# Delta recurrence: applying the inverse to (r - Kg S) in each step instead of forming the product of Kg and the inverse

## The chip, the cores and the metric

The kernel runs on one core of a Trainium2 chip, as one program. The metric is the device time of one execution in microseconds, taken as the median over several runs. A core has a matrix engine (TensorE, "PE" in the profile, whose weight loads are listed apart as "PEld"), a vector engine (VectorE, "DVE"), a scalar engine (ScalarE, "ACT"), GpSimd ("POOL") and SyncE ("SP"), which here only starts DMA transfers. In this kernel every engine works through its own instructions in the order in which the program wrote them, and the engines wait for each other through semaphores. The products stand in PSUM until VectorE or ScalarE takes them away.

## The reference

One decoder layer with three gated branches is computed for a prompt of 1024 tokens and for 8 decode tokens. From h = RMSNorm(x) one wide projection (1024 to 7688 columns) feeds a gated delta-rule branch, a spatial-gating branch and a cross-attention branch; each is projected back, gated and merged, and an output projection, a residual and a norm follow. The change is in the delta-rule branch. Its chunked form, cut to what matters here:

```python
L = where(strict, einsum('id,jd->ij', k_beta, k) * decay, 0.0)
Tinv = triangular_solve(eye + L, eye)           # the inverse
u = Tinv @ (v * beta)
w = Tinv @ (k_beta * exp(gc))
attn = where(causal, q @ k.T * decay, 0.0)
def step(S, xs):                                # over the chunks, S is the state
    v_new = u_i - w_i @ S
    o = qd_i @ S + attn_i @ v_new
    S = S * gl_i + kd_i.T @ v_new
    return S, o
```

There are 4 heads with keys and values of 128 columns. Since u - w S = Tinv (v beta - (k beta exp(gc)) S), the inverse may be applied before or after the difference is formed.

## The kernel before

All activations are kept transposed: features on partitions, tokens along the free dimension. The projections are products of 128x128 weight blocks with 344 tokens, done three times (high x high, high x low, low x high part) for accuracy. A *job* is one block of 128 output features: `w_next` takes its split weights and starts the load of the block three jobs ahead, then three groups follow (`h_group`, `mm3`, L272 to L282), each of 24 matmuls into one of two PSUM banks ("pj"), and each group's result is taken away, mostly by ScalarE (L957).

The order of the work is written by hand. The class `Streams` holds side streams, which are Python generators. `mm3` calls `tick` after every sixth matmul, and a tick advances each side stream to its next `yield`; `yield n` lets n more ticks pass first. So the instructions of side streams come to stand between the matmuls of the projections, in the order of the ticks. `plan_a` (L205 to L210) lists the jobs of the first stage: k, v and q of head 0, then more of branch A and B and some gates, up to the last gate of head 3's row. The recurrence is the side stream `delta_all` (L949): `gates_gen`, then `delta_gen(h)` for the heads 0 to 3, one after the other. After the last job of `plan_a` stands `run.until(lambda: ("delta", 3) in done)` (L994), which ticks on without any matmuls until head 3 has ended. Only then the next stage is written: loads of the memory input and of small tables on SP's queue (L1010 to L1026), `mem_norm` (L291), and the jobs of `plan_c`, which begins with two gates, a gate and the first w_mem_kv block.

`delta_gen(h)` works in 8 chunks of 128 tokens. It transposes k by chunks (L756 to L766) and, out of the same PSUM tiles, forms Kg = k exp(gc) with tokens on partitions; it forms the decayed products LA (L780), the right-hand side r from v (L810), and the transposes of q for its norm (L817); `gcb` holds exp(gc) over tokens along the free dimension, and L827 turns it into q exp(gc). GpSimd inverts the small diagonal blocks (L835), and TensorE with VectorE builds the whole inverse U from them (L854 to L888). Then come the product of Kg and U (L890 to L896) and the recurrence over chunks (L900 to L922): y, the new state Sn, and the output. After the chunks the output is normed (L924 to L931), transposed back (L935), gated, and stored to `ya_d` (L946).

The scaling of beta and of the norms is folded into other factors: r, kd and LA carry them.

Of the kernel before, what the change touches and what calls it, by code (L numbers as in the profile page):

```python
# [12 lines left out]
F32 = mybir.dt.float32  # L13
F32R = mybir.dt.float32r
I32 = mybir.dt.int32
AF = mybir.ActivationFunctionType
ALU = mybir.AluOpType
AX = mybir.AxisListType
PSUM = bass.MemoryType.PSUM
DRAM = bass.MemoryType.DRAM  # L20

P = 128
D = 1024
T = 1024
# [5 lines left out]
H = 4  # L30
CC = 8
# [59 lines left out]


class Streams:
    """Interleaves the emission of side streams (generators) with the main stream of matrix products."""

    def __init__(self):
        self.items = []
# [21 lines left out]
def tile_mixer_step(ctx: ExitStack, tc: tile.TileContext, a):  # L119
    nc = tc.nc  # L120
    V, S, G, PE, SP = nc.vector, nc.scalar, nc.gpsimd, nc.tensor, nc.sync
# [25 lines left out]
    def dl():  # L147
        return ps.tile([P, 512], F32, tag="dl", name="dl", bufs=4)
# [41 lines left out]
        p = in_.shape[0]  # L190
        PE.transpose(out, in_, ident[:p, :p])  # L191

    # ---- weights: loaded three jobs ahead, split one job ahead
    w_in_v = a["w_in"].rearrange("(k p) n -> p k n", p=P)
    w_kv_v = a["w_mem_kv"].rearrange("(k p) n -> p k n", p=P)
    w_br_v = [a[n].rearrange("(k p) n -> p k n", p=P) for n in ("w_br_a", "w_br_b", "w_br_c")]
# [90 lines left out]
        for n in range(NS):  # L287
            evac(n, *h_group(w, n))

    # ---- RMSNorm of the inputs, transposed and split  # L290
    def mem_norm(np_, srcs, g_bc, dst_h, dst_l):  # L291
        ss = np_.tile([P, 2], F32, tag="nss", name="mss")
        r = np_.tile([P, 2], F32, tag="nrs", name="mrs")
# [168 lines left out]

    run.add(norm_gen())

    # ---- scratch in DRAM for branch parts that wait for their turn
    ya_d, bv_d, ug_d, yc_d, yb_d = (
        [dr.tile([P, NT], F32, name=f"{n}{h}") for h in range(H)] for n in ("ya", "bv", "ug", "yc", "yb")
    )
# [5 lines left out]
    def bc4(x):  # L474
        return x.unsqueeze(2).to_broadcast([P, x.shape[1], P])

    # ---- branch A
    dst = ExitStack()
    kq_t, v_t, kq_s = {}, {}, {}
    xraw = {}  # L480
# [59 lines left out]
    for n in range(4):  # L540
# [10 lines left out]
    dp = scoped(dst, "dp")  # L551
# [3 lines left out]
        out=mask, in_=mask, pattern=[[1, P]], compare_op=ALU.is_ge, fill=NEG, base=0, channel_multiplier=-1  # L555
# [3 lines left out]
        out=ut, in_=ones, pattern=[[1, P]], compare_op=ALU.is_ge, fill=0.0, base=0, channel_multiplier=-1  # L559
# [4 lines left out]
    U = dp.tile([P, CC, P], F32, name="U")  # L564
# [5 lines left out]
    beta = dp.tile([P, H, 9], F32, name="beta")  # L570
    g = dp.tile([P, H, 9], F32, name="g")
    gc = dp.tile([P, H, CC], F32, name="gc")
    eg = dp.tile([P, H, CC], F32, name="eg")
    egl = dp.tile([P, H, CC], F32, name="egl")
    ekd = dp.tile([P, H, CC], F32, name="ekd")
    gcd = dr.tile([32, P], F32, name="gcd")
# [12 lines left out]
    def gates_gen():  # L589
        sel = dp.tile([16, 8], F32, name="sel")  # L590
        V.tensor_tensor(out=sel, in0=ident[:16, 0:8], in1=ident[:16, 8:16], op=ALU.add)
        yield
        t = tp()
        for i in range(9):
            PE.matmul(t[:, i * 8:(i + 1) * 8], lhsT=ab[:, i * P:(i + 1) * P], rhs=sel, start=True, stop=True)
        abt = dp.tile([P, 2, H, 9], F32, name="abt")
        V.tensor_copy(out=abt, in_=t[:, :72].rearrange("p (i t h) -> p t h i", i=9, t=2))
        yield
        S.activation(out=beta, in_=abt[:, 0], func=AF.Exp, scale=-1.0)
        z = abt[:, 1]  # L600
        V.tensor_tensor(out=z, in0=z, in1=al_bc[:, 1].unsqueeze(2).to_broadcast([P, H, 9]), op=ALU.add)
        e1 = dp.tile([P, H, 9], F32, name="e1")
        V.tensor_scalar(out=e1, in0=z, scalar1=-1.0, scalar2=None, op0=ALU.mult)
        V.tensor_tensor(out=e1, in0=z, in1=e1, op=ALU.min)
        S.activation(out=e1, in_=e1, func=AF.Exp)
        S.activation(out=al_bc[:, 0], in_=al_bc[:, 0], func=AF.Exp)
        yield
        V.tensor_scalar(out=beta, in0=beta, scalar1=1.0, scalar2=None, op0=ALU.add)
        V.reciprocal(out=beta, in_=beta)
        s1 = dp.tile([P, H, 9], F32, name="s1")  # L610
        V.tensor_scalar(out=s1, in0=e1, scalar1=2.0, scalar2=None, op0=ALU.add)
        V.reciprocal(out=s1, in_=s1)
        V.tensor_tensor(out=s1, in0=s1, in1=e1, op=ALU.mult)
        s2 = dp.tile([P, H, 9], F32, name="s2")
        V.tensor_tensor(out=s2, in0=s1, in1=s1, op=ALU.mult)
        V.tensor_scalar(out=e1, in0=s2, scalar1=2.0 / 17.0, scalar2=None, op0=ALU.mult)
        yield
        for m in range(15, 1, -2):
            V.scalar_tensor_tensor(out=e1, in0=e1, scalar=2.0 / m, in1=s2, op0=ALU.add, op1=ALU.mult)
            if m == 9:  # L620
                yield
        V.scalar_tensor_tensor(out=e1, in0=e1, scalar=2.0, in1=s1, op0=ALU.add, op1=ALU.mult)
        V.scalar_tensor_tensor(out=z, in0=z, scalar=0.0, in1=e1, op0=ALU.max, op1=ALU.add)
        V.scalar_tensor_tensor(
            out=g, in0=z, scalar=-1.0, in1=al_bc[:, 0].unsqueeze(2).to_broadcast([P, H, 9]), op0=ALU.mult, op1=ALU.mult
        )
        gp = dp.tile([P, H, CC], F32, name="gp")
        V.tensor_copy(out=gp, in_=g[:, :, :CC])
        gpf = gp.rearrange("p h c -> p (h c)")
        yield 3  # L630
        t = tp()
        PE.matmul(t[:, 0:32], lhsT=ut, rhs=gpf, start=True, stop=True)
        PE.matmul(t[:, 32:64], lhsT=ones, rhs=gpf, start=True, stop=True)
        PE.matmul(t[:32, 128:256], lhsT=gpf, rhs=ut, start=True, stop=True)
        gcr = dp.tile([32, P], F32, name="gcr")
        S.copy(out=gcr, in_=t[:32, 128:256])
        SP.dma_start(out=gcd, in_=gcr)
        sbg = dr.tile([NB, 2, H], F32, name="sbg")
        SP.dma_start(out=sbg[:, 0], in_=beta[:NB, :, 8])
        SP.dma_start(out=sbg[:, 1], in_=g[:NB, :, 8])  # L640
        tg = t[:, 32:64].rearrange("p (h c) -> p h c", h=H)
        V.tensor_copy(out=gc, in_=t[:, 0:32].rearrange("p (h c) -> p h c", h=H))
        V.tensor_tensor(out=ekd, in0=tg, in1=gc, op=ALU.subtract)
        S.activation(out=egl, in_=tg, func=AF.Exp)
        S.activation(out=eg, in_=gc, func=AF.Exp)
        S.activation(out=ekd, in_=ekd, func=AF.Exp)
        sbb = dp.tile([P, NB, 2, H], F32, name="sbb")
        SP.dma_start(out=sbb, in_=sbg.rearrange("b t h -> (b t h)").partition_broadcast(P))
        done.add("gates")
        yield 5  # L650
        V.tensor_copy(out=bs, in_=sbb[:, :, 0].rearrange("p b h -> p h b"))
        S.activation(out=as_, in_=sbb[:, :, 1].rearrange("p b h -> p h b"), func=AF.Exp)
        done.add("sgates")
# [79 lines left out]
    def delta_gen(h):  # L733
# [3 lines left out]
        kq, vt = kq_t[h], v_t[h]  # L737
# [5 lines left out]
        gcb = dp.tile([P, CC, P], F32, tag="gcb", name="gcb")  # L743
        SP.dma_start(out=gcb, in_=gcd[h * CC:(h + 1) * CC].rearrange("c i -> (c i)").partition_broadcast(P))
        E = dp.tile([P, CC, P], F32, tag="E", name="E")
        ss = sm.tile([P, 2, CC], F32, tag="ss", name="ss")
        Kg = dp.tile([P, CC, P], F32, tag="Kg", name="Kg")
        kd = dp.tile([P, CC, P], F32, tag="kd", name="kd")
        r = dp.tile([P, CC, P], F32, tag="r", name="r")
        ssk = sm.tile([P, CC], F32, tag="ssk", name="ssk")  # L750
# [5 lines left out]
        for cs in halves:  # L756
            t = dl().rearrange("p (c n) -> p c n", c=4)
            kt.append(t)
            for c in range(4):
                cc = cs.start + c  # L760
                transpose(t[:, c], kq[:, 0, cc * P:(cc + 1) * P])
            for c in range(4):
                cc = cs.start + c
                S.activation(out=junk(), in_=t[:, c], func=AF.Square, accum_out=ss[:, 0, cc:cc + 1])
            V.tensor_tensor(out=Kg[:, cs], in0=t, in1=bc4(eg[:, h, cs]), op=ALU.mult)
            yield 1  # L766
        for c in range(CC):
            V.scalar_tensor_tensor(
# [49 lines left out]
        for cs in halves:  # L818
            t = dl().rearrange("p (c n) -> p c n", c=4)
            for c in range(4):  # L820
                cc = cs.start + c
                transpose(t[:, c], qg[:, cc])
            for c in range(4):
                cc = cs.start + c
                S.activation(out=junk(), in_=t[:, c], func=AF.Square, accum_out=ss[:, 1, cc:cc + 1])
            yield 1
        V.tensor_tensor(out=gcb, in0=qg, in1=gcb, op=ALU.mult)  # L827
        yield
        ssq = sm.tile([P, CC], F32, tag="ssq", name="ssq")
# [57 lines left out]
            PE.matmul(t1[lo_, c], lhsT=p2[hi_, c], rhs=U[hi_, c, hi_], start=True, stop=True)  # L887
        V.tensor_copy(out=U[lo_, :, hi_], in_=t1[lo_])  # L888
        yield 1
        wT = Kg  # L890
        for cs in halves:
            t = dl().rearrange("p (c n) -> p c n", c=4)
            for c in range(4):
                PE.matmul(t[:, c], lhsT=Kg[:, cs.start + c], rhs=U[:, cs.start + c], start=True, stop=True)  # L894
            S.mul(out=wT[:, cs], in_=t, mul=-1.0)
            yield  # L896
        o_t = r
        sso = sm.tile([P, CC], F32, tag="sso", name="sso")
        Sc = None
        for c in range(CC):  # L900
            t = dl()[:, :P]
            PE.matmul(t, lhsT=U[:, c], rhs=r[:, c], start=True, stop=(c == 0))  # L902
            if c:
                PE.matmul(t, lhsT=wT[:, c], rhs=Sc, start=False, stop=True)  # L904
            y = dp.tile([P, P], F32, tag="y", name="y", bufs=2)
            V.tensor_copy(out=y, in_=t)  # L906
            yield
# [13 lines left out]
            Sc = Sn  # L921
# [73 lines left out]
    dst.close()  # L995
    xst.close()

    # ---- memory keys and values, spatial mixing of branch B, branch C
    cst = ExitStack()
    kvp = scoped(cst, "kvp", side="right")  # L1000
    kTh = kvp.tile([P, H, MEM], F32R, name="kTh")
# [339 lines left out]
        run.add(load_y(y1p, ya_d, 0))  # L1341
    cst.close()

    # ---- branch projections, gated and merged
    mp = scoped(mst, "mp")
    merged = mp.tile([P, KT, NT], F32, name="merged")
    y2st = ExitStack()
# [67 lines left out]
            m_split(0, slice(0, KT - 1))  # L1415
        merge(i)

    # ---- output projection, residual, final norm
    fg_bc = op.tile([P, D], F32, name="fg_bc", bufs=1)
    SP.dma_start(out=fg_bc, in_=a["final_norm_g"].partition_broadcast(P))  # L1420
    sel8 = op.tile([16, NB], F32, name="sel8", bufs=1)
# [88 lines left out]
```

## Time and profile before

| what | value |
|---|---|
| median of 3 runs (lowest, highest) | 1151.32 us (1150.09, 1153.52) |
| span of the profiled execution | 1148.6 us |
| PE busy | 1119.7 us, 97% |
| PEld busy | 1074.8 us, 94% |
| DVE busy | 609.7 us, 53% |
| ACT busy | 411.9 us, 36% |
| POOL busy | 214.1 us, 19% |
| L894, product of Kg and the inverse | 64 matmul instructions, 275 ns each by the median |
| last store of branch A (L946) | issued at 546.88 us |

The profiled execution is given by its span, from its first to its last instruction; the runs' times also hold what lies around it. A row of the view in order of time gives start, duration, engine, line, operation, tiles ("out<-in"), shape and number of instructions merged; a bracket at its end gives the idle time ahead of it and what ended it. "PEq", "SPq" and the like are the engines' sequencers. An f32 product of 128x128 by 128x128 shows as two matmul instructions. In rows of the view by stretches the columns are busy times (and instruction counts) of PE, PEld, DVE, ACT and POOL, then the granted clock of TensorE, the busy share of the DMA engines and GB/s. In rows by line the numbers are the shortest, median and longest duration in ns, then the first and last start.

### The profile page before, as it was taken

What the parts mean: (1) busy time and instruction counts of PE and PEld (TensorE: products, weight loads), DVE (VectorE), ACT (ScalarE), POOL (GpSimd) and SP (SyncE); (2) the same over time, 40 slices, a digit from 0 to 9 for tenths busy, and PEclk for the clock granted to TensorE, in tenths of its full rate; (3) what the DMA queues carried; (4) which work ended last, traced back from release to release, by engine and by line L of the source; (5) the groups of instructions that cost most, each with busy time, mean ns of one, the idle gap of its engine ahead of it and who ended that gap; (6) DMA issues with size and microseconds to landing.
All of it is one profiled execution on the core that took longest, in us unless ns stands there. A gap on an engine that the chain in (4) does not pass through costs nothing.

```text
span 1148.6 us, 19257 instructions
## 1 busy us (share of the span) xinstructions
PE 1119.7 (97%) x7609; PEld 1074.8 (94%) x7609; DVE 609.7 (53%) x1512; ACT 411.9 (36%) x891; POOL 214.1 (19%) x392
## 2 busy tenths in 40 slices
PE   5999999999999999999999999999999999999997
PEld 4989999999999999999999999989999999998884
DVE  6754654655465546513277432655545246786554
ACT  5434233333331333333344333545445321232232
POOL 1060715070507050600034000101101000000000
PEclk9999999999999999999999999999999999999999
DMA  8104420341143114422654556543432465662221
GB/s 250 39 20 97 132 63 23 117 129 46 40 125 104 45 41 126 124 79 77 200 138 137 166 170 186 159 118 93 146 114 74 145 195 176 212 213 100 83 93 57
DMA packets 153772, 133.53 MB, mean 116 GB/s; under 512 B 20941, under 2 KB 134922, under 8 KB 153674
## 3 DMA queue, kind: packets, MB, share of 16 engines
q1 hardware_dynamic: 72242, 89.82, 24.5%
q10 hardware_dynamic: 81440, 42.49, 13.7%
q8 instruction: 60, 0.98, 0.3%
q14 instruction: 30, 0.25, 0.1%
HBM read 100.74 MB, written 31.64 MB: 115 GB/s over the span
## 4 chain that ended last, share of the span: by engine, by line
PE 90%; DVE 4%; DMA 2%; ACT 2%; issue 1%; SPq 1%; ACTq 0%; DVEq 0%
PE pj L275 56%; PE dl L275 20%; PE tp L191 2%; PE dl L191 2%; PE dl L784 1%; DMA raw<-w_in 1%; DMA stg<-ya 1%; PE dl L894 1%; PE tp L1094 1%; PE dl L918 1%; PE dl L909 1%; PE dl L902 1%; PE dl L904 1%; PE dl L917 1%; DVE wlo L253 1%
## 5 line engine op out<-in xcount | busy, mean ns | idle before, releaser
L275 PE MATMUL pj<-hTh,whi 128*128 128x344 f32 (+1 forms) x1456 | 280.7, 327 | 3.1 <-DVE ql L155 1.1
L275 PE MATMUL pj<-hTh,wlo 128*128 128x344 f32 (+1 forms) x1456 | 277.5, 325 | 0.0
L275 PE MATMUL pj<-hTl,whi 128*128 128x344 f32 (+1 forms) x1456 | 272.3, 322 | 0.0
L275 PEld LDWEIGHTS pj<-hTh,whi 128*128 128x128 f32 x1456 | 232.4, 190 | 5.9 <-ACT hTh L393 1.5
L275 PEld LDWEIGHTS pj<-hTh,wlo 128*128 128x128 f32 x1456 | 235.1, 189 | 1.4 <-issue 0.8
L275 PEld LDWEIGHTS pj<-hTl,whi 128*128 128x128 f32 x1456 | 234.3, 188 | 1.1 <-DVE hTl L394 0.2
L253 DVE TENSOR_TENSOR wlo<-raw,whi 128x1024 fp32r<-128x1024 f32 (+1 forms) x91 | 102.5, 1126 | 51.7 <-ACT whi L250 44.2
L250 ACT CAST whi<-raw 128x1024 fp32r<-128x1024 f32 (+1 forms) x92 | 86.2, 937 | 81.5 <-PE dl L275 64.8
L957 ACT COPY stg<-pj 128x344 f32<-128x344 f32 x72 | 32.1, 446 | 108.0 <-PE pj L275 107.6
L838 POOL TENSOR_TENSOR itmp<-X,Lt 128x60 f32<-128x60 f32 (+24 forms) x124 | 43.7, 352 | 125.7 <-DMA Lt<-ld 116.5
L1184 POOL TENSOR_TENSOR kvt<-kvt,qb 128x1024 f32<-128x1024 f32 x8 | 19.2, 2419 | 210.7 <-DMA qb<-qd 130.9
L275 PE MATMUL dl<-yh,whi 128*128 128x344 f32 x288 | 57.3, 321 | 0.0
L275 PE MATMUL dl<-yh,wlo 128*128 128x344 f32 x288 | 57.3, 321 | 0.0
L275 PE MATMUL dl<-yl,whi 128*128 128x344 f32 x288 | 57.1, 320 | 0.0
L275 PEld LDWEIGHTS dl<-yh,whi 128*128 128x128 f32 x288 | 47.8, 188 | 0.0
L275 PEld LDWEIGHTS dl<-yh,wlo 128*128 128x128 f32 x288 | 47.7, 188 | 0.0
L275 PEld LDWEIGHTS dl<-yl,whi 128*128 128x128 f32 x288 | 47.6, 188 | 0.0
L844 POOL TENSOR_TENSOR X<-X,itmp 128x60 f32<-128x60 f32 (+24 forms) x124 | 43.7, 353 | 9.7
L531 ACT COPY xraw<-pj 128x344 f32<-128x344 f32 (+2 forms) x38 | 16.3, 430 | 66.4 <-PE pj L275 63.1
L906 DVE COPY y<-dl 128x128 f32<-128x128 f32 x32 | 9.3, 291 | 55.3 <-PE dl L904 34.4
L1367 DVE TENSOR_TENSOR stg<-dl,stg 128x344 f32<-128x344 f32 x48 | 24.7, 515 | 18.1 <-PE dl L275 18.1
L503 POOL TENSOR_TENSOR kq<-kq,cvt 128x512 f32<-128x512 f32 x24 | 32.6, 1358 | 1.9
(378 smaller groups left out, 1591.9 us busy)
## 6 DMA issues: line engine op xcount, KB each, us to landing
raw<-w_in ACTq DMA_DIRECT2D x57, 512.0 KB
gate<-stg SPq DMA_DIRECT2D x23, 516.0 KB
stg<-gate SPq DMA_DIRECT2D x23, 516.0 KB
x<-x_prompt SPq DMA_DIRECT2D x8, 512.0 KB
raw<-w_mem_kv ACTq DMA_DIRECT2D x8, 512.0 KB
kvt<-cache_mem_k SPq DMA_DIRECT2D x16, 256.0 KB
kvt<-cache_mem_v SPq DMA_DIRECT2D x16, 256.0 KB
wor<-w_out SPq DMA_DIRECT2D x8, 512.0 KB
```

The costliest lines, as they stand in the source:

```text
L191: PE.transpose(out, in_, ident[:p, :p])
L250: S.copy(out=hi, in_=raws[i])
L253: eng.tensor_tensor(out=lo, in0=raws[i], in1=f32(hi), op=ALU.subtract)
L275: PE.matmul(out, lhsT=w, rhs=r, start=(i == 0), stop=(i == len(ops) - 1))
L503: G.tensor_tensor(out=d[:, cs], in0=d[:, cs], in1=o, op=ALU.add)
L531: S.copy(out=raw[:, 3 + sl.start:3 + sl.stop], in_=o)
L784: PE.matmul(t, lhsT=kq[:, 0, sl], rhs=kq[:, :, sl], start=True, stop=True)
L838: G.tensor_tensor(out=tm, in0=X[:, 0:m, j:j + 1].to_broadcast([P, m, n]), in1=Lt[:, j:j + 1, j + 1:32].to_broadcast([P, m, n]), op=ALU.mult,)
L844: G.tensor_tensor(out=X[:, 0:m, j + 1:32], in0=X[:, 0:m, j + 1:32], in1=tm, op=ALU.subtract)
L957: project("gate", i, lambda n, sl, o: S.copy(out=t[:, sl], in_=o))
L1184: G.tensor_tensor(out=kts[hb], in0=kts[hb], in1=qb[:, hb * 4:hb * 4 + 4].unsqueeze(2).to_broadcast([P, 4, 2, P]), op=ALU.mult,)
L1367: V.tensor_tensor(out=sg[:, sl], in0=o, in1=sg[:, sl], op=ALU.mult)
```

## The change

Kg times the inverse (wT) is no longer formed. In each chunk but the first, the program now forms Kg S from the state, subtracts it from r in place, and applies the inverse U once to the difference. Kg is needed for that with features on partitions, so it is no longer made out of the transposed k with a factor per partition (`eg`), but out of k itself with the factor `gcb` along the free dimension, in one instruction over all chunks, ahead of the one that turns `gcb` into q exp(gc). The subtraction is followed by a `yield` of its own. The docstring of a class and comments are dropped as well, which changes nothing in the program.

```diff
-    eg = dp.tile([P, H, CC], F32, name="eg")
...
-        S.activation(out=eg, in_=gc, func=AF.Exp)
...
-        Kg = dp.tile([P, CC, P], F32, tag="Kg", name="Kg")
...
-            V.tensor_tensor(out=Kg[:, cs], in0=t, in1=bc4(eg[:, h, cs]), op=ALU.mult)
             yield 1
...
+        kg = dp.tile([P, CC, P], F32, tag="Kg", name="kg")
+        V.tensor_tensor(
+            out=kg, in0=kq[:, 0, :T].rearrange("p (c i) -> p c i", c=CC), in1=gcb, op=ALU.mult
+        )
+        yield 1
         V.tensor_tensor(out=gcb, in0=qg, in1=gcb, op=ALU.mult)
         yield
...
-        wT = Kg
-        for cs in halves:
-            t = dl().rearrange("p (c n) -> p c n", c=4)
-            for c in range(4):
-                PE.matmul(t[:, c], lhsT=Kg[:, cs.start + c], rhs=U[:, cs.start + c], start=True, stop=True)
-            S.mul(out=wT[:, cs], in_=t, mul=-1.0)
-            yield
         o_t = r
         sso = sm.tile([P, CC], F32, tag="sso", name="sso")
         Sc = None
         for c in range(CC):
+            if c:
+                t = dl()[:, :P]
+                PE.matmul(t, lhsT=kg[:, c], rhs=Sc, start=True, stop=True)
+                V.tensor_tensor(out=r[:, c], in0=r[:, c], in1=t, op=ALU.subtract)
+                yield
             t = dl()[:, :P]
-            PE.matmul(t, lhsT=U[:, c], rhs=r[:, c], start=True, stop=(c == 0))
-            if c:
-                PE.matmul(t, lhsT=wT[:, c], rhs=Sc, start=False, stop=True)
+            PE.matmul(t, lhsT=U[:, c], rhs=r[:, c], start=True, stop=True)
             y = dp.tile([P, P], F32, tag="y", name="y", bufs=2)
             V.tensor_copy(out=y, in_=t)
             yield
```

## Prediction

> **What bounds the kernel now.** First the page: busy shares and the chain that ended last; then the busy time by stretches around the recurrence.
>
> ```profile
> span 1148.6 us, 19257 instructions
> PE 1119.7 (97%) x7609; PEld 1074.8 (94%) x7609; DVE 609.7 (53%) x1512; ACT 411.9 (36%) x891; POOL 214.1 (19%) x392
> ...
> PE 90%; DVE 4%; DMA 2%; ACT 2%; issue 1%; SPq 1%; ACTq 0%; DVEq 0%
> ...
> 500.00:550.00 50.00, 50.00 (x433) 48.89 (x433) 14.98 (x39) 16.71 (x45) 0.00 (x0) 1.00 0.25 80
> ```
>
> TensorE runs through: 90% of the chain is its own, and in the 50 us that hold the last head's recurrence it has no gap, VectorE being busy for 14.98 and ScalarE for 16.71. So work off TensorE is free as long as projections lie between the recurrence's steps; TensorE work counts in full. The next view is TensorE's order of time around the product of Kg and the inverse and through one chunk (start, duration; one f32 product is two passes, so x2):
>
> ```profile
> 511.73 0.48 PE L275 MATMUL pj<-hTh,wlo 128*128 128x344 f32 x2
> 512.04 1.05 PE L894 MATMUL dl<-U,Kg 128*128 128x128 f32 x8
> 512.85 1.19 PE L275 MATMUL pj<-hTh,wlo 128*128 128x344 f32 x6
> ...
> 518.29 0.38 PE L902 MATMUL dl<-r,U 128*128 128x128 f32 x2
> 518.51 0.39 PE L904 MATMUL dl<-S,Kg 128*128 128x128 f32 x2
> 518.65 1.20 PE L275 MATMUL pj<-hTh,wlo 128*128 128x344 f32 x6
> 519.69 0.38 PE L909 MATMUL dl<-y,kd 128*128 128x128 f32 x2
> 519.91 0.39 PE L917 MATMUL dl<-S,gcb 128*128 128x128 f32 x2
> 520.13 0.39 PE L918 MATMUL dl<-y,LA 128*128 128x128 f32 x2
> ...
> 521.29 0.38 PE L902 MATMUL dl<-r,U 128*128 128x128 f32 x2
> ```
>
> A chunk takes two ticks: L902 and L904, six projection matmuls, then L909, L917, L918 and six more. It repeats after 521.29 - 518.29 = 3.00 us.
>
> **Where the last head ends.** The recurrence advances one yield per tick, and ticks come only out of the projections' loop, one per six matmuls. Two questions decide: do the heads follow one another without slack, and how many ticks are left when the last one ends? The loads and stores of SP's queue, then TensorE's rows with the first weight load of the next stage:
>
> ```profile
> 205.47 0.32 SPq L946 DMA_DIRECT2D ya<-agt  x1
> 205.88 0.43 SPq L744 DMA_DIRECT2D gcb<-gcd  x1
> ...
> 432.69 0.35 SPq L946 DMA_DIRECT2D ya<-agt  x1
> 433.14 0.38 SPq L744 DMA_DIRECT2D gcb<-gcd  x1
> ...
> 546.88 0.32 SPq L946 DMA_DIRECT2D ya<-agt  x1
> ```
>
> ```profile
> 545.47 0.60 PE L191 MATMUL dl<-ident,r 128*128 128x128 f32 x4
> 545.82 1.20 PE L275 MATMUL pj<-hTh,wlo 128*128 128x344 f32 x6
> 546.87 1.43 PE L275 MATMUL pj<-hTh,whi 128*128 128x344 f32 x8
> ...
> 550.68 1.42 PE L275 MATMUL pj<-hTh,whi 128*128 128x344 f32 x8
> ...
> 550.89 0.38 ACTq L242 DMA_DIRECT2D raw<-w_mem_kv  x1
> ```
>
> Head 0's store is followed 0.41 us later by head 1's first load, head 2's 0.45 us later by head 3's: a head starts where the one before it ends, and a yield added in head 0 moves all four. The last head's second output transpose stands at 545.47, its store is emitted a tick later, at the end of that group (546.87). One group of 24 matmuls, four ticks, follows, up to 550.68. That group is the last of the stage, since a job loads the weights three jobs ahead and the first w_mem_kv tile is the fourth entry of the next plan. Behind it the program empties the recurrence with nothing between its steps. **The slack is four ticks.** Those 24 matmuls take 550.68 - 546.87 = 3.81 us, 0.159 each, and a chunk's five products take 3.00 - 12 x 0.159 = 1.09, 0.22 each.
>
> **The change, part by part.**
>
> Removed: 32 products (L894) at 0.22 make **7.0 us** of TensorE, fully on the path (the eight passes at 512.04 push the next projection matmul from about 512.05 to 512.85). Also, per head, two Kg products on VectorE, two ScalarE negations, and eg once:
>
> ```profile
> L765 DVE TENSOR_TENSOR Kg<-dl,eg x8: 691/692/693, 97.4 to 438.8; 128x512 f32<-128x512 f32 x8
> ...
> L895 ACT ACTIVATE Kg<-dl x8: 597/598/600, 171.2 to 515.0; 128x512 f32<-128x512 f32 x8
> ...
> L827 DVE TENSOR_TENSOR gcb<-kq,gcb x4: 1212/1268/1324, 118.6 to 460.9; 128x1024 f32<-128x1024 f32 x4
> ```
>
> Added: kg per head, the twin of L827 (1.27 us), against 2 x 0.69 saved, so VectorE is even there; and seven subtractions per head of a 128x128 out of PSUM. The trace has no such subtraction; its cost lies between the copy L906 (0.28 to 0.29) and the three-operand L912 (0.35, both below): I take 0.31. These 28 x 0.31 = 8.7 us of VectorE hide under projections; where VectorE is held by a weight split (1.2 us) a step may come late, 0 to 2 us in all, 0.5 taken. Behind a waiting subtraction stand VectorE's weight splits, which TensorE needs a job later; behind a waiting U r stand the projection matmuls themselves. The seven products with the state per head stay, with kg for wT, in a tick of their own: no TensorE time either way. No DMA is added; stores and first loads of heads 1 to 3 move later with the heads.
>
> Ticks: two yields of the removed halves go; seven yields come, and kg's `yield 1`, which costs two ticks. That is +7 a head, **+28 at the end of the last head, against a slack of four: 24 ticks run bare.** A chunk now has steps A (kg S, subtract), B (U r, copy), C (kd y, new state). Counting back from the store: one tick for it, two for the transposes, two skipped, three of rsqrt, three for each chunk. Behind the last projection matmul stand B and C of chunk 2 and all of chunks 3 to 7, then rsqrt, scaling and transposes.
>
> What a bare step costs: the one place where VectorE released this chain late, then the new state and the chain's end:
>
> ```profile
> 176.65 0.28 DVE L914 COPY S<-dl 128x128 f32<-128x128 f32 x1
> ...
> 176.98 0.30 PEld L904 LDWEIGHTS dl<-S,Kg 128*128 128x128 f32 x2 [0.32 <-DVE S L914]
> 176.98 0.49 PE L904 MATMUL dl<-S,Kg 128*128 128x128 f32 x2
> ...
> 177.57 0.28 DVE L906 COPY y<-dl 128x128 f32<-128x128 f32 x1
> ...
> 520.11 0.35 DVE L912 SCALAR_TENSOR_TENSOR S<-S,egl,dl 128x128 f32<-128x128 f32 x1 [0.89 <-PE dl L909]
> ...
> 541.77 1.23 DVE L931 TENSOR_TENSOR r<-r,ro 128x1024 f32<-128x1024 f32 x1
> ```
>
> From the copy's end (176.93) to TensorE 0.05, the product 0.49 (0.39 where weights were loaded ahead), some 0.04 to VectorE (L909 ends near 520.07, L912 starts at 520.11): 0.58 plus the VectorE operation. A is 0.88, B 0.86, C 0.92, so **2.66 us a bare chunk**, bounds 2.4 (product 0.39) and 2.9. To chunk 7's last product: B 0.81 and C 0.92 of chunk 2, A and B of chunk 7 and four whole chunks 12.4, then 0.05 and 0.44 (519.69 to 520.13) up to L918: 14.6. From the last L918 of before, 520.13 + 6 x 3.00 = 538.13, to L931's end, 543.00, is 4.85: the squares' sum, rsqrt, scaling. With 0.05 and the eight transposes (545.47 to 545.82, 0.35 for four) the tail is 20.2 us. Under projections the same 29 products cost 0.22 each, 6.3, and the transposes 0.7: 7.0. So the bare tail adds **13.2 us** (12 to 15).
>
> Two things follow the tail. **The clock.** Windows as the profile records them, and TensorE in them (after PE, PEld, DVE, ACT and POOL the next number is the granted clock):
>
> ```profile
> 71.96:75.37 3.41, 3.41 (x27) 3.17 (x26) 0.88 (x3) 1.47 (x2) 3.25 (x4) 1.00 0.46 133
> 75.37:78.78 3.41, 3.41 (x14) 3.41 (x13) 3.38 (x4) 1.29 (x3) 3.33 (x3) 0.50 0.00 0
> ...
> 72.22 2.17 PE L595 MATMUL tp<-sel,ab 16*128 16x8 f32 x18
> ...
> 75.06 2.23 PE L275 MATMUL pj<-hTh,wlo 128*128 128x344 f32 x8
> ```
>
> A window with 2.17 us of tiny products was followed by one at half clock, in which eight matmuls took 2.23 instead of 1.43: 1.56 times. In the bare chain the array works 5 x 0.22 of 2.66 us, about 40%, and then pauses for nearly 5 us. A bare product would go from 0.49 to 0.76, 0.8 us a chunk. I expect half the chunks slow, 2 us, and as much at the restart: **+4** (0 to 7).
> The Trainium skill, "TensorE: Matmul & The Clock Gate", section "HAM oscillation — how this bites in real kernels", asks for no idle gaps of TensorE over about 3.4 us; the chain's gaps are under 1 us, so by that rule only the last pause would cost clock, which is rival (2). The window at 71.96 does not bear the rule out: TensorE shows as busy for all of it, and yet the clock fell.
>
> **SP's queue.** Behind the last store stand the next stage's loads, in the program's order:
>
> ```profile
> 552.43 7.09 SPq L297 DMA_DIRECT2D x<-mem_prompt  x2
> ...
> 559.80 1.06 ACT L302 ACTIVATE xn<-x 128x1024 f32<-128x1024 f32 x1 [4.66 <-DMA x<-mem_prompt]
> ...
> 560.85 0.43 ACT L957 COPY stg<-pj 128x344 f32<-128x344 f32 x1
> ```
>
> Before, the store went out 3.8 us ahead of the next stage (550.68); now it goes out about 1 us behind its start (last transposes to store: 1.4 us, less their 0.36). The memory input landed 12.9 us after the store, and ScalarE waits for it in order, with the projections' eviction (560.85) queued behind it. The group evicted there ended at 550.68 + 7.62 = 558.30, its successor at 562.12, where TensorE needs that bank again: the eviction had 0.84 us to spare. 4.8 us later it leaves TensorE waiting about 4. If the loads, which the tail no longer crowds, land faster, it is 0: **+2.5** taken.
>
> The sum: -7.0 + 0.5 + 13.2 + 4 + 2.5 = **+13.2**. It is made against the profiled execution, 1148.6 of span; the median of the runs, 1151.32, is 2.7 longer, what lies around the span with it. 1148.6 + 13.2 + 2.7 = 1164.5, **1164** predicted.
>
> **The rivals.** (1) Forecast: bare tail, half the chain at half clock, loads late: 1164, chance 0.40. (2) The clock holds through the bare chain and falls only in the pause of 4.85 us for rsqrt and scaling: the clock term is 2, the time 1162. For it: the products at 72.22 move 8 columns, these 128, so this array is busier than that one was. Chance 0.15. (3) Bare tail alone: the clock holds and the loads come in time, -7.0 + 0.5 + 13.2 = +6.7, 1158. Chance 0.20. (4) Faster: the 28 ticks find room (a head's start that absorbs them, or TensorE work behind the store that I do not see) and the saved products remain: -6.5, 1145. It decides from 24 more spare ticks; against it stand the 0.41 us between heads and the four ticks. 0.08. (5) The tail's steps go at 60% of my price, as the engines overlap more than the rows show: its 13.2 would shrink to about 7, with no followers +0.5, 1152. 0.06. (6) The extra handshake also fails under cover: VectorE late by 0.3 us in most of the 23 covered chunks, +6 on the forecast, 1170. Against it: A asks 0.39 + 0.04 + 0.31 + 0.05 = 0.79 us and gets 0.22 + 6 x 0.159 = 1.17. 0.11.
>
> **How the numbers follow.** The range, 1156 to 1172, runs from (3) with a tail of 12 to (1) with the upper ends, -7.0 + 2 + 15 + 7 + 4 = +21; it leaves out (4) and (5). A measurement of this kernel tells about 0.3%, 3.5 us, from no change. Slower by more: (1), (2), (3), (6), 0.86; within: (5), 0.06; faster: (4), 0.08.
>
> **What would show it.** No L894; in the covered chunks a step every six projection matmuls and a period of 4.0 us (18 x 0.159 + 1.09). L946's fourth store after the last projection of its stage instead of 3.8 us before. A stretch of about 20 to 23 us in which TensorE has only recurrence products, with VectorE as releaser, 2.7 to 3.4 us a chunk, some clock at 0.5. Then ScalarE's wait for the memory input with TensorE idle behind it. Wrong if projections stand between the last head's chunks to its end, or if that stretch is under 14 us.

## The result, and the profile after

The changed kernel takes **1169.68 us** (median of 4 runs, 1166.65 to 1172.42) against 1151.42 for the kernel before (4 runs). The ratio is 1.0147, with a 95% interval of 1.0127 to 1.0167: 16.9 us slower (14.6 to 19.2); the two medians by themselves lie 18.3 us apart. The forecast was 1164, the range 1156 to 1172. The profiled execution of the changed kernel took 1169.76 us, with a span 19.4 us longer than before, so its rows are read against a difference of 19.4.

The page of the changed kernel: span, busy times and the granted clock in 40 slices.

```profile
span 1168.0 us, 19171 instructions
...
PE 1127.6 (97%) x7545; PEld 1078.7 (92%) x7545; DVE 620.9 (53%) x1536; ACT 407.0 (35%) x881; POOL 227.6 (19%) x392
...
PEclk9999999999999999998799999999999999999999
```

TensorE issues 64 matmuls fewer (7545 against 7609) and is busy for 7.9 us more; VectorE has 24 instructions more. Two slices of the clock, the 19th and the 20th (about 526 to 584 us), stand out. The cause is seen in TensorE's order of time around the end of head 3 (start, duration, then line, tiles, shape, instructions, and in brackets the idle time ahead):

```profile
540.57 0.48 PE L275 MATMUL pj<-hTh,wlo 128*128 128x344 f32 x2
540.88 0.38 PE L901 MATMUL dl<-r,U 128*128 128x128 f32 x2
...
543.45 0.49 PE L901 MATMUL dl<-r,U 128*128 128x128 f32 x2 [0.38 <-DVE r L898]
...
550.20 0.79 PE L901 MATMUL dl<-r,U 128*128 128x128 f32 x2 [0.38 <-DVE r L898]
...
553.83 0.79 PE L901 MATMUL dl<-r,U 128*128 128x128 f32 x2 [0.38 <-DVE r L898]
...
559.66 0.63 PE L915 MATMUL dl<-y,LA 128*128 128x128 f32 x2
564.79 1.97 PE L191 MATMUL dl<-ident,r 128*128 128x128 f32 x8 [4.50 <-DVE r L928]
566.41 2.44 PE L275 MATMUL pj<-hTh,whi 128*128 128x344 f32 x8
568.68 1.43 PE L275 MATMUL pj<-hTl,whi 128*128 128x344 f32 x8
```

Up to 540.88 a chunk repeats after 3.96 us (kg S at 535.75 and 539.71; forecast 4.0). The last projection matmul of the stage is followed by U r of chunk 2 and by no further projection until 566.41: from 540.88, **25.53 us** of bare recurrence, which before did not exist at all. Step B of chunk 2 and all that comes behind it stand bare, as forecast. A bare chunk takes 543.45 - 540.88 = 2.57 us at first and 553.83 - 550.20 = 3.63 us later, with the same wait of 0.38 for VectorE in both; what has grown is the product, 0.49 to 0.79. The same kernel by stretches (busy times of PE, PEld, DVE, ACT and POOL, then the granted clock):

```profile
540.90:544.60 3.70, 2.55 (x15) 1.79 (x15) 1.22 (x4) 0.98 (x4) 0.00 (x0) 1.00 0.02 4
544.60:559.90 15.30, 12.25 (x46) 9.89 (x45) 4.12 (x14) 3.18 (x13) 0.00 (x0) 0.50 0.08 35
559.90:566.40 6.50, 2.00 (x10) 1.71 (x10) 3.85 (x15) 1.47 (x4) 0.00 (x0) 0.50 0.31 91
```

The clock is at half not only in the last pause but through 15.3 us of products. TensorE then starts the next stage slow: the group at 566.41 needs 2.27 us to its successor, where such a group needs 1.27 (before: 548.14 - 546.87).

What TensorE waited for in the changed kernel (us in total, times, longest):

```profile
PE dl L906 <- DVE y L903: 2.3, 6, 0.4
PE dl L901 <- DVE r L898: 1.9, 5, 0.4
PE tp L631 <- DVE gp L627: 1.7, 1, 1.7
...
PE pj L275 <- ACT stg L954: 1.2, 1, 1.2
PE tp L684 <- DVE kqn L676: 0.9, 1, 0.9
PE dl L873 <- DVE pn L867: 0.8, 1, 0.8
```

The eleven waits of L901 and L906 are those of the bare chunks; under projections the chain made TensorE wait once, for 0.2 us in head 0 (L897 at 176.48). L954 is the eviction behind the late memory input. L684, a product of the decode sample's side stream, did not wait before, and neither did L873.

A balance, by one point in the program: the first projection of the next stage starts at 550.68 before and at 566.41 after, 15.7 us later. At 540.88 the changed kernel had done all projections of the stage, 9.8 us ahead of before. Of these 9.8, 7.0 are the removed products and 7.0 the 29 products and eight transposes that now stand behind, by the forecast's prices; so 4.2 us had been lost on the way; what they are is taken up below. Behind 566.41 the slow restart (1.0) and the wait for L954 (1.2) follow, 17.9 of the 19.4 us with them; most of the rest is a later wait for VectorE (L155, 2.3 us against 1.1).

### The profile page after: what moved, and what is told of

It reads as the page before. It is cut to its first block, busy times and chain, and to the rows that moved or that the text cites. A ratio compares the mean times of both kernels' runs of the same rounds, so it can differ in the third digit from the quotient of the medians.

```text
span 1168.0 us, 19171 instructions
## 1 busy us (share of the span) xinstructions
PE 1127.6 (97%) x7545; PEld 1078.7 (92%) x7545; DVE 620.9 (53%) x1536; ACT 407.0 (35%) x881; POOL 227.6 (19%) x392
## 4 chain that ended last, share of the span: by engine, by line
PE 85%; DVE 5%; DMA 4%; POOL 3%; issue 2%; ACT 1%; SPq 1%; ACTq 0%; POOLq 0%; DVEq 0%
PE pj L275 51%; PE dl L275 20%; PE tp L191 2%; PE dl L191 2%; POOL itmp L839 1%; POOL X L845 1%; PE dl L780 1%; PE dl L906 1%; PE dl L901 1%; DMA raw<-w_in 1%; DMA stg<-ya 1%; PE dl L915 1%; PE dl L897 1%; DVE wlo L253 1%; PE dl L914 1%
## 5 line engine op out<-in xcount | busy, mean ns | idle before, releaser
L839 POOL TENSOR_TENSOR itmp<-X,Lt 128x60 f32<-128x60 f32 (+24 forms) x124 | 51.1, 412 | 174.7 <-DMA Lt<-ld 165.5
L954 ACT COPY stg<-pj 128x344 f32<-128x344 f32 x72 | 32.1, 446 | 114.9 <-PE pj L275 114.5
L1181 POOL TENSOR_TENSOR kvt<-kvt,qb 128x1024 f32<-128x1024 f32 x8 | 19.2, 2421 | 212.4 <-DMA kvt<-cache_mem_v 131.8
L845 POOL TENSOR_TENSOR X<-X,itmp 128x60 f32<-128x60 f32 (+24 forms) x124 | 50.1, 404 | 9.7
L916 ACT COPY r<-dl 128x128 f32<-128x128 f32 x32 | 8.5, 266 | 80.8 <-PE dl L915 72.5
L1364 DVE TENSOR_TENSOR stg<-dl,stg 128x344 f32<-128x344 f32 x48 | 24.7, 514 | 18.2 <-PE dl L275 18.1
```

What stands on the lines that cost most here:

```text
L839: G.tensor_tensor(out=tm, in0=X[:, 0:m, j:j + 1].to_broadcast([P, m, n]), in1=Lt[:, j:j + 1, j + 1:32].to_broadcast([P, m, n]), op=ALU.mult,)
L845: G.tensor_tensor(out=X[:, 0:m, j + 1:32], in0=X[:, 0:m, j + 1:32], in1=tm, op=ALU.subtract)
L954: project("gate", i, lambda n, sl, o: S.copy(out=t[:, sl], in_=o))
L1181: G.tensor_tensor(out=kts[hb], in0=kts[hb], in1=qb[:, hb * 4:hb * 4 + 4].unsqueeze(2).to_broadcast([P, 4, 2, P]), op=ALU.mult,)
L1364: V.tensor_tensor(out=sg[:, sl], in0=o, in1=sg[:, sl], op=ALU.mult)
```

## The experiments

Each is timed against runs of the kernel before on the same chip; medians of that lie between 1152.6 and 1153.5.

**One step fewer: subtraction and U r in one tick.** From the changed kernel:

```diff
-        yield 1          # behind kg
...
-                yield    # behind the subtraction
```

> The changed kernel without its two new yields: the subtraction and the product with the inverse stand in one tick, and kg in the tick of the product behind it. A head then takes two ticks fewer than before, so no step runs bare. But the product with the inverse now stands right behind the product with the state, and TensorE waits for the subtraction in each of 28 chunks with nothing in between: 0.39 + 0.04 + 0.31 + 0.05 - 0.22 = 0.57 us each, 16 us in all. Theory (the cost of the change is the bare tail, which is a matter of ticks): projections go on between the chunks of the last head up to its end, the granted clock is 1.00 there, and the time is 1151 - 7 + 16 = 1160, with 28 waits for the subtraction in the trace. Rival (the added step costs the same wherever it stands, through VectorE): about the changed kernel's 1170, with the same gap of TensorE at the end of the last head.

Measured: 1169.63, ratio 1.0149 (1.0132 to 1.0165). This is the rival's time, 10 us above the theory's 1160. But its trace shows the mechanism of the theory, larger. First TensorE in a covered chunk, then a row of its waits:

```profile
301.80 0.38 PE L896 MATMUL dl<-S,kg 128*128 128x128 f32 x2
302.56 0.49 PE L899 MATMUL dl<-r,U 128*128 128x128 f32 x2 [0.38 <-DVE r L897]
302.81 1.19 PE L275 MATMUL pj<-hTh,wlo 128*128 128x344 f32 x6
```

```profile
PE dl L899 <- DVE r L897: 10.8, 28, 0.5
```

The two products hold TensorE for 302.81 - 301.80 = 1.01 us, where two back to back took 0.36 before (518.29 to 518.65). 28 times 0.65 is 18.2 us, without the 7.0 it is +11.2. The bare tail is gone: projections stand among the chunks up to the last transposes. So the tick of its own is worth its price, and 1170 was reached on another road than rival (6) has. The rest of the 17 us is waits elsewhere (2.3 us for LA's product, L780, for which 1.0 was waited before; behind it the granted clock is 0.50 from 223.5 to 226.8) and was not taken apart.

**The ticks alone.** The arithmetic of before with the changed kernel's yields; no product is added or removed:

```diff
+        yield 1          # where kg is formed
...
-            yield        # the two halves of Kg U
...
+            if c:
+                yield    # ahead of U r
```

> The kernel before with its own arithmetic, product of Kg and the inverse included, but with the yields of the changed kernel: two yields of the halves go, one empty yield comes ahead of each chunk but the first, and yield 1 ahead of the scaling of q. Theory (ticks alone): 28 ticks more, the same bare tail with two handshakes a chunk instead of three; from the changed kernel's tail a handshake for the subtraction, about 1.0 us at half clock, goes from each of 5 chunks, so a tail of about 20.5 instead of 25.5 us. Time 1151 + 20.5 - 7 + 2 = 1167, slower than before though no work was added. Rival (the cost is the added product's handshake and VectorE's subtractions): 1151 within 3.

Measured: 1165.31, ratio 1.0103 (1.0090 to 1.0117), 11.9 us for ticks alone. Two chunks in its tail, and the tail by stretches:

```profile
545.30 0.39 PE L904 MATMUL dl<-r,U 128*128 128x128 f32 x2
...
547.10 0.39 PE L904 MATMUL dl<-r,U 128*128 128x128 f32 x2
```

```profile
543.50:554.40 10.90, 8.61 (x62) 7.33 (x60) 3.83 (x13) 4.17 (x17) 0.00 (x0) 1.00 0.12 48
554.40:560.60 6.20, 1.61 (x9) 1.58 (x9) 3.90 (x17) 1.49 (x4) 0.00 (x0) 0.69 0.33 98
```

The slack of four ticks and what lies beyond it are right: 17.1 us of recurrence (543.54 to 560.64) run bare. Its chunks have one handshake fewer, 1.80 us each, and here the clock **held** through the chain and fell only in the pause, as rival (2) said of the changed kernel.

**Hold the clock in the bare tail.** The changed kernel with extra products of 344 columns into a spare PSUM bank, whose result nobody reads, while TensorE waits for VectorE:

```diff
+                fill(3)  # behind kg S, ahead of U r
...
+            fill(3)      # ahead of kd y
...
+            fill(1)      # at a chunk's end
...
+        fill(24)         # in the last pause
```

> The changed kernel with products into the bare tail whose result nobody reads: three of 344 columns behind the step with the subtraction, three behind the step with the inverse, one behind the step with the new state, 24 ahead of the output transposes of the last head. They are to keep the array busy in the waits (0.6 us a step) without standing in the way. Theory (a good part of the tail is the clock that falls in it): the granted clock stays at 1.00 from 540 to 570, a bare chunk goes from 3.63 back to about 2.6 to 2.7 us, and the tail from 25.5 to 20 to 21 us; time about 1164. Rival (the handshakes alone make the tail, the clock does not matter): the tail stays at 25 us or grows by the products.

Measured: 1164.07, ratio 1.0097 (1.0073 to 1.0120), 5.8 us less than the changed kernel by the medians of the ratios. The tail's first row, one chunk, and the first projection behind the tail; then the clock:

```profile
539.56 0.38 PE L908 MATMUL dl<-r,U 128*128 128x128 f32 x2
...
546.60 0.49 PE L903 MATMUL dl<-S,kg 128*128 128x128 f32 x2
...
549.27 0.49 PE L903 MATMUL dl<-S,kg 128*128 128x128 f32 x2
...
559.97 1.51 PE L275 MATMUL pj<-hTh,whi 128*128 128x344 f32 x8
```

```profile
544.60:554.50 9.90, 9.90 (x65) 8.14 (x65) 3.51 (x13) 2.55 (x10) 0.00 (x0) 1.00 0.13 53
554.50:560.00 5.50, 4.92 (x35) 4.64 (x34) 3.72 (x17) 1.50 (x4) 0.00 (x0) 1.00 0.37 107
```

The chunk takes 2.67 us (forecast 2.66), the tail 559.97 - 539.56 = 20.4 (forecast 20.2). So 25.5 - 20.4 = 5.1 us of the tail, and 1.0 at the restart, are the clock's, and more work on TensorE made the kernel faster.

**Cover for half of the bare ticks.** The changed kernel with one gate's job, which is 12 ticks of projections, moved from the next stage to the end of this one:

```diff
-    ... + gates(7),
+    ... + gates(8),
...
-        plan_c += gates(1) + [("kv", j)]
+        plan_c += (gates(1) if j < 7 else []) + [("kv", j)]
```

> The changed kernel with one gate block more in the first plan instead of two: 12 of the 24 bare ticks are covered. Theory (bare tail, most of it at half clock): four of the 5.33 bare chunks come under projections, each worth 3.6 less 1.1 us, while the pause of about 5 us for the norm stays bare: 1170 - 10 = 1160, between the changed kernel and e3_after_g9. Rival (a fixed cost at the border of the two stages, like the late loads): no lower than 1168.

Measured: 1159.19, ratio 1.0052 (1.0038 to 1.0065). The tail's first row and the first projection behind it, then the clock:

```profile
557.47 0.38 PE L901 MATMUL dl<-r,U 128*128 128x128 f32 x2
...
567.96 1.43 PE L275 MATMUL pj<-hTh,whi 128*128 128x344 f32 x4
```

```profile
557.40:562.00 4.60, 3.29 (x20) 2.34 (x18) 1.64 (x6) 1.11 (x5) 0.00 (x0) 1.00 0.00 0
562.00:568.00 6.00, 1.66 (x9) 1.66 (x9) 3.91 (x15) 2.38 (x5) 0.00 (x0) 0.53 0.57 189
```

12 ticks of cover shorten the tail from 25.5 to 10.5 us and the kernel by 10.9 (0.0095 of 1152). The bare chain that is left is over in 4.6 us, before the clock falls.

**Cover for all of it, and its control.** The same with two gates (24 ticks), in the changed kernel and in the kernel before:

```diff
-    ... + gates(7),
+    ... + gates(9),
...
-        plan_c += gates(1) + [("kv", j)]
+        plan_c += (gates(1) if j < 6 else []) + [("kv", j)]
```

> The changed kernel with two gate blocks more in the last head's row of the first plan and two fewer among the memory key and value blocks: the same work in another order, 24 ticks more under projections in the first stage. Theory (bare tail): 28 ticks now meet a slack of 28, the recurrence ends under projections, and what is left of the change is the removed product less some waits: 1144 to 1150, below the control e4_before_g9 by 2 to 7. Rival (cost of the added step under cover): it stays slower than e4_before_g9, at 1160 or above.

> The control of e3_after_g9: the kernel before with the same two gate blocks moved into the first plan. Both theories: the work is the same and TensorE is busy at both places, so 1151 within 3. If it is faster or slower than that, moving the gates has a worth of its own, to be taken off e3_after_g9.

Measured: the control 1152.37, ratio 0.9995 (0.9985 to 1.0006), so the move alone is worth nothing. The changed kernel 1154.83, ratio 1.0017 (1.0007 to 1.0027). This missed: with the tail gone it should have kept the saving of the products. It has no bare tail, but waits of TensorE that neither the kernel before nor the control has, these two among them:

```profile
PE pj L275 <- ACT stg L954: 2.5, 1, 2.5
...
PE tp L684 <- DVE kqn L676: 0.9, 1, 0.9
```

**What the product's removal is worth.** The kernel before without the product of Kg and the inverse and its negation; the tile keeps Kg, so that part of the result is left out; all yields stay:

```diff
-            t = dl().rearrange("p (c n) -> p c n", c=4)
-            for c in range(4):
-                PE.matmul(t[:, c], lhsT=Kg[:, cs.start + c], rhs=U[:, cs.start + c], start=True, stop=True)
-            S.mul(out=wT[:, cs], in_=t, mul=-1.0)
             yield
```

> The kernel before without the product of Kg and the inverse and without its negation: Kg itself goes into the recurrence, so that part of the computation is left out; all yields stay. It prices the saving by itself. Theory: 32 products at 0.22 us, 1151 - 7 = 1144. Rival (the product stood in time that TensorE has anyway): 1149 to 1151.

Measured: 1147.03, ratio 0.9949 (0.9931 to 0.9966), 5.9 us less (3.9 to 8.0). The forecast's 7.0 lies inside. So the changed kernel with full cover lost some 8 us of another kind.

**Where those 8 us went.** Three variants of the covered kernel: kg formed earlier, behind kd, and its tick dropped (A); the same with the tick kept where it was (B); A with kg on GpSimd (C).

```diff
+        kg = dp.tile([P, CC, P], F32, tag="Kg", name="kg")
+        V.tensor_tensor(out=kg, ...)       # A, B; G.tensor_tensor in C
         yield from rsqrt_slow(nk, ssk, "nk")
...
-        kg = dp.tile([P, CC, P], F32, tag="Kg", name="kg")
-        V.tensor_tensor(out=kg, ...)
-        yield 1                            # A, C; kept in B
         V.tensor_tensor(out=gcb, in0=qg, in1=gcb, op=ALU.mult)
```

A:

> e3_after_g9 with kg formed earlier, behind the scaled keys and ahead of the sample's work, without a tick of its own. In the changed kernel's trace kg (1.31 us) stands between the small steps of the sample's norm on VectorE, and TensorE waits 0.9 us for them in the last head and then has 3.4 us at half clock. Theory: 1 to 4 us below e3_after_g9, so 1143 to 1148. Rival (those waits are chance of one execution): the same as e3_after_g9 within 1.

B:

> e7 with the tick of kg (yield 1, two ticks a head) put back where the change has it; kg itself stays early, behind kd. Against e3 it differs only in the place of kg on VectorE, against e7 only in eight ticks up to the last store. If e3's loss (1.0017 against 0.9973 of e7, about 5 us) came from kg on VectorE among the sample's small steps, this is as fast as e7: ratio 0.997, about 1149, and the sample's product L684-L688 no longer waits 0.9 us in the last head. If it came from the eight ticks (store and loads late at the border, ScalarE's eviction L954 behind the memory input), it is as slow as e3: ratio 1.002, about 1155, with a wait of TensorE for L954 of some 2.5 us. Half and half would be 1152.

C:

> e7 with kg formed on GpSimd instead of VectorE, at the same place (GpSimd waits there for the load of Lt). Theory that VectorE's order still costs e7 something: 0.5 to 2 us faster than e7, about 1147 to 1148.5, ratio 0.996. Rival: nothing of e7's time hangs on it, or GpSimd's longer product delays its own loop L843-L849 and the head behind it: 1149 to 1152, ratio 0.997 to 1.000.

Measured: A 1148.94, ratio 0.9973 (0.9958 to 0.9987); B 1152.39, ratio 0.9992 (0.9978 to 1.0005); C 1150.16, ratio 0.9966 (0.9953 to 0.9979; its chip's kernel before stood at 1153.53). B lies between: by the medians of the ratios it is 2.9 us faster than the covered kernel, from which it differs in kg's place on VectorE, and 2.2 slower than A, from which it differs in the eight ticks. The intervals of A and B overlap, those of B and the covered kernel just do not, and kg in its old place without its tick was not run: both sizes are estimates, and they hold for this order of taking apart. The covered kernel with kg in its old place, then B, at the same product of the sample:

```profile
481.13 2.47 PE L684 MATMUL tp<-kqn,st 128*128 128x2 f32 x16 [0.90 <-DVE kqn L676]
```

```profile
481.44 1.84 PE L684 MATMUL tp<-kqn,st 128*128 128x2 f32 x16
```

In B the sample's product waits in no head; with the eight ticks the store and the loads behind it still come late at the border, and TensorE waits for L954 for 2.5 us as in the row above. In the profiled executions of A and C the wait for L954 is gone. But there L684 waits again, 1.0 us, in the second head instead of the last, and it is not kg that stands in its way. In C, whose kg is not on VectorE at all, it is the scaling of q:

```profile
241.15 1.30 DVE L827 TENSOR_TENSOR gcb<-kq,gcb 128x1024 f32<-128x1024 f32 x1
```

```profile
243.41 1.95 PE L684 MATMUL tp<-kqn,st 128*128 128x2 f32 x16 [1.02 <-DVE kqn L676]
```

So the cost is that of an instruction of 1.3 us among the sample's small steps on VectorE, kg or another, and the ticks decide which one falls there and in which head. C against A shows no gain that can be told, so with kg early no gain of a free VectorE is seen. A and C beat both kernels, by 0.3%: half to two thirds of what the removed products are worth.

## Why the prediction came out as it did

The sign, the place and the chain of causes were right; the sum, +13.2, was 3.7 us short of the measured 16.9 (5.1 short of the 18.3 between the medians). By its own terms:

- **The product, -7.0.** The kernel without it gives -5.9 (-8.0 to -3.9).
- **Four ticks of slack, 24 bare.** Right to the step: the tail begins with step B of chunk 2. The ticks alone cost 11.9 us with no work added, and taking away 12 or 24 of them gives 10.9 and 15.0 us back.
- **The bare tail, 20.2 us long, +13.2.** With the clock held it is 20.4, a chunk 2.67 against 2.66. A bare step priced as VectorE's operation plus 0.58 holds (with the operations named, 0.31, 0.28 and 0.35, its three steps add up to 2.68; the sum took 2.66).
- **The clock, +4 ("half the chunks slow, 2 us, and as much at the restart").** This was mis-sized: 5.1 in the tail and 1.0 behind it. The clock fell 3.7 us into the chain, and nearly all of the rest ran at half. Rival (2), that it would hold through the chain, falls with the row at 544.60 and its 0.50. The Trainium skill's rule ("TensorE: Matmul & The Clock Gate", "HAM oscillation — how this bites in real kernels"), no idle gap over about 3.4 us, would have kept the clock up there: no gap in the chain's rows is longer than 0.38, and so the measurement decides against it as a sufficient condition.
- **Loads late, +2.5.** Measured 1.2.
- **VectorE late under cover, +0.5.** The second wrong term: kg's place alone makes about 2.9 us (the covered kernel against B).

The rows for the loads, from the order of time of the changed kernel:

```profile
567.58 0.32 SPq L943 DMA_DIRECT2D ya<-agt  x1
...
578.70 1.06 ACT L302 ACTIVATE xn<-x 128x1024 f32<-128x1024 f32 x1 [6.84 <-DMA x<-mem_prompt]
...
580.23 1.53 PE L275 MATMUL pj<-hTh,whi 128*128 128x344 f32 x8 [1.23 <-ACT stg L954]
```

The store goes out 1.17 us behind the restart (forecast about 1), but ScalarE has the memory input 11.1 us after it instead of 12.9, and a stage that starts at half clock needs its banks later.

The rows for VectorE, the subtractions by line (shortest, median and longest in ns, first and last start) and kg of the last head in order of time:

```profile
L898 DVE TENSOR_TENSOR r<-r,dl x28: 275/286/290, 177.3 to 557.1; 128x128 f32<-128x128 f32 x28
```

```profile
479.28 1.31 DVE L824 TENSOR_TENSOR kg<-kq,gcb 128x1024 f32<-128x1024 f32 x1
```

The subtractions take 0.29 us and make no covered product wait. But "VectorE is even there" counted kg's time against the Kg products saved and did not ask where kg stands: at 479.28, among the small steps of the sample on whose result L684 waits. Of the 4.2 us lost ahead of the tail, 0.9 are this wait and about 1.2 the 3.4 us at half clock behind it (an estimate, at the prediction's 1.56 times); 0.8 are L873; the other way, TensorE waits 1.0 us for LA's product (L784) before and not in the changed kernel. By stretches, the changed kernel, then B:

```profile
482.00:485.00 3.00, 3.00 (x19) 3.00 (x19) 2.09 (x8) 0.00 (x0) 2.61 (x6) 0.69 0.00 0
```

```profile
482.00:485.00 3.00, 3.00 (x24) 3.00 (x24) 2.11 (x11) 0.08 (x1) 2.53 (x7) 1.00 0.07 28
```

Another 1.5 us of the 4.2 are not the change's. They are there at 97.94, where the changed kernel starts the group that before starts at 96.39, and up to that point the change has only dropped `eg`. What they come from is the clock of the first stage. L631 (L632 before), for which TensorE waited 1.7 us against 0.2 before, starts as long behind the tiny products (L595 before, L594 after) in both kernels, 83.93 - 72.22 = 11.71 and 83.63 - 71.90 = 11.73 us. Before, then after:

```profile
83.93 0.41 PE L632 MATMUL tp<-gp,ut 128*128 128x32 f32 x2 [0.22 <-DVE gp L628]
```

```profile
71.90 2.17 PE L594 MATMUL tp<-sel,ab 16*128 16x8 f32 x18
...
83.63 0.52 PE L631 MATMUL tp<-gp,ut 128*128 128x32 f32 x2 [1.75 <-DVE gp L627]
```

So VectorE sets the time of L631, and the longer wait by itself costs nothing. Before, the clock fell behind the tiny products, and TensorE came to L631 late; in the changed kernel it held there (1.00 from 75.3 to 78.8), TensorE came early and waited, and the clock fell behind the wait (0.51 from 83.7 to 90.6). In the profiled executions of all twelve kernels L631 starts 11.7 to 11.8 us behind these products. In eight the clock falls behind them and L631 waits 0.2; in four (the changed kernel, one step fewer, the ticks alone, full cover) it holds and L631 waits 1.7 to 1.8. So what the prediction read in the window at 71.96 does not happen each time.

With the measured sizes (2.9 for VectorE) the sum is -5.9 + 2.9 + 13.4 + 6.1 + 1.2 = +17.7 against 16.9 (14.6 to 19.2).

Of the rivals, (3) falls with the clock, (5) with the 2.57 to 3.63 us of a bare chunk, (4) with the missing cover: it needed the 24 ticks, and with them alone the kernel is still not faster. (6) gave the nearest number and is refuted by the rows: under cover one step waits, for 0.2 us. What stays open: by the ratios, whose intervals overlap, A is still 2.8 us slower than the kernel without the product. Its L684 wait (1.0) and the half clock behind it (1.2 by the estimate above) would make most of that, but this is read in one execution and was not tested.

## What to carry to other kernels

When work is interleaved by hand, count the steps as well as the work: a step added to a serial side stream is free only while main work is left to stand between its steps, and the slack is read where the side stream's last instruction stands against the main stream's last. Price an uncovered chain at the handshake (here 0.58 us plus VectorE's operation a step), and reckon that the clock may fall in it: it did here with three handshakes a chunk and not with two. An instruction that is even in busy time is not even in effect: look at what stands behind it on its engine at that place, and remember that an added tick moves other instructions into such places too.

## What the hardware showed

The clock fell without any long gap. In the changed kernel's chain TensorE shows as busy for 2.55 of 3.70 us (69%), with no gap over 0.38, and went to 0.50 after that stretch; in the chain of the ticks-only kernel, busy for 8.61 of 10.90 (79%), it stayed at 1.00. The share of busy time alone is not the rule, though. Later in the changed kernel TensorE shows as busy for 59% of a stretch as long as one at half clock, and the clock holds through it and behind it:

```profile
773.28:776.69 3.41, 2.01 (x14) 1.69 (x13) 2.86 (x10) 0.56 (x2) 0.00 (x0) 1.00 0.00 0
```

What the clock goes by is left open here. Filling the waits with products that nobody reads paid 5.8 us. A short disturbance does it too: in the changed kernel a wait of 0.9 us at products of two columns was followed by 3 us at a mean clock of 0.69, and in B, where that wait was missing, the same stretch ran at 1.00. Five more profiled executions have this wait, 0.9 to 1.0 us long, and half clock follows in each: 0.50 over 3.3 us in A (244.9 to 248.2), C, the filled tail and the half cover, over 6.7 us in the full cover (482.4 to 489.1). The wait is not needed for it: with one step fewer the clock fell once behind the same products without one (0.50 from 360.0 to 363.3).
